# Moving the softmax attention's query projection from filling work into a pass of seven half-size products

## The chip, the cores and the metric

The kernel runs on one core of one Trainium2 chip. A core has engines that run side by side and wait for each other by semaphores: TensorE (PE, matrix products, with PEld for its weight loads), VectorE (DVE), ScalarE (ACT), GpSimd (POOL), and SyncE (SP), whose queue issues the transfers between DRAM and the on-chip memory SBUF. Products land in PSUM, in eight banks. The metric is the device time of one execution in microseconds (us). Less is better.

## The reference, cut to what matters

One encoder layer over 1024 tokens of width 1024, in float32. An input projection gives everything that the two attention branches need; branch A is gated linear attention (GLA) in both directions, branch B is softmax attention over a window (SWA).

```python
h = _rms_norm(x, norm_mix_g[l])
proj = h @ w_in[l]
(g_q, g_k, g_v, g_r, g_lr_f, g_lr_b,
 s_q, s_k, s_v, gate_a, gate_b) = jnp.split(proj, split_at, axis=-1)
y_gla = _gla_branch(g_q, g_k, g_v, g_r, ...) @ w_o_gla[l]
y_swa = _swa_branch(s_q, s_k, s_v, ...) @ w_o_swa[l]
merged = sigmoid(gate_a) * y_gla + sigmoid(gate_b) * y_swa
x = x + merged @ w_out[l]
x = x + (silu(ff_gate) * ff_up) @ w_ffn_out[l]
```

The change is about four parts of `proj`: `g_v` (GLA values, 1024 columns), `s_q` (SWA queries, 1024 columns), `s_k` with `s_v` (SWA keys and values, 256 columns each), and `g_r` (1024 columns, used only when branch A's output is gated).

## The kernel before, in words

**Precision.** Every large product is made of three matmuls in the fast type fp32r: each operand is split into a high part (ScalarE copies it to fp32r) and a low part (VectorE subtracts the high part from the original), and high x high, high x low and low x high are summed in PSUM. One matmul takes a 128x128 block of one operand and streams 512 columns of the other. `wunit` (L67) makes one weight unit of 128x512: SP loads 256 KB, ScalarE copies (L70), VectorE subtracts (L72).

**Stages, in the order of the program.** First come projections by a scheme with seven instead of eight half-size products (0 to 249.6 us in the profile). Then `values()` (L516 to L561) makes `g_v` the same way: seven products of `vproduct` (L474 to L483), each of four weight units on four PSUM banks, three matmuls each, so 48 matmuls a product and 336 in all, on line L482. Two groups of four banks take turns: `A` from the `ch` banks, `B` from the `mm` banks. The finished blocks are split into high and low and stored to DRAM by `vkeep` (L488).

Then the GLA stage (325.8 to about 555 us) runs in slots. A table `at` (L862 on) says which step of which chunk (`g_gates`, `g_powers`, `g_scores`, `g_out`, `g_back_out`, `g_turn`, and `k_norm` of the softmax keys) stands in which slot. There are 4 heads of 8 chunks, slots 0 to 45. The order of TensorE's instructions is the order in which the program writes them; the other engines' order is left to the scheduler. Between the steps `slot` (L212) calls `fill(n)`, which puts in n matmuls of a list `dense` of projections that nothing waits for soon: `skv` (192 matmuls), `sq0` and `sq1` (192 each, the softmax queries), and `r0` to `r7` (48 each), 960 in all. The fillings split their weights by `wunit`: one unit for 12 matmuls of `proj_t` (skv, sq0, sq1), and one for 24 of `proj_f` (r0 to r7). Finished blocks leave PSUM by ScalarE (`proj_t`, L189, 8 copies of 128x512 in 192 matmuls) or by VectorE (`proj_f_out`, L128, 2 in 48).

The SWA stage (about 555 to 738 us) has a table `todo` of the same kind: for each of 16 units of 4 heads, `a_load`, `a_prep` (normalise and rotate the queries, VectorE), `a_turn` (L970, transposes), `a_scores` (products, maximum, exponential, and on GpSimd the division, L1008), and two slots later `a_probs` and `a_out`. It goes on filling, and `fill(1 << 30)` after it puts in what is left. From 738 us on come the output projections and the feed-forward part, which the change does not touch.

**How many matmuls a slot gets.** GLA: `fill(24)` first, then 24 in slots 0 and 1, 16 in slots 2 and 3, 12 in slots 4 to 35, 8 in slots 36 to 43, 18 in slots 44 and 45 (L878). SWA: 26 in slots 0 and 1, 15 in slots 2 to 18, 18 after (L1084).

**What the steps of a chunk do on the small engines.** `g_scores` (L719) scales two query blocks by a decay (`q2f`, `q2b`, VectorE, L746) and splits the scores into `sh` (VectorE, L750) and `sl` (VectorE, L751). `k_norm` (L834) normalises and rotates the keys of one tile of 128 tokens, eight calls. `g_back_out` (L787) ends with a pair of scaled outputs `ob` (ScalarE, L805), which `g_turn` (L807) transposes on TensorE (L811), copies and stores (L815).

Of the kernel before, what the change touches and what calls it, by code (L numbers as in the profile page):

```python
# [8 lines left out]
F32 = mybir.dt.float32  # L9
# [5 lines left out]
P = 128  # L15
# [15 lines left out]
def body(tc, i, out):  # L31
    nc = tc.nc
    with ExitStack() as root:
# [102 lines left out]

        def next_unit():
            while plan and len(ready) <= AHEAD:
                ready.append(wunit(plan.pop(0)))
            return ready.pop(0)  # L140

        def proj_f(name, m):
            plan.extend(i["w_f"][m, u] for u in range(2))
# [17 lines left out]
        def proj_t(name, n):  # L161
            for s in range(2):
                plan.extend(i["w_t"][n, k] for k in range(KT))
# [287 lines left out]
        def x_last(f):  # L451
# [9 lines left out]
                 "12": ("xr00", "xr20", "xr21", "xr10"), "u": ("wr2", "wr2", "wr2", "rsl"), "p": ("ws",) * 4}  # L461

# [5 lines left out]

        def vload(q, k):
            nc.sync.dma_start(out=vtile(q, k), in_=i["w_t"][int(q[0]) - 1, 4 * int(q[1]) - 4 + k])  # L470
# [4 lines left out]
        def vproduct(ys, w, x, start, stop, after):  # L475
            for kk in range(4):
# [6 lines left out]
                after(kk)  # L483

# [31 lines left out]
        def values():  # L516

            A = [chtile((P, HT)) for _ in range(4)]
# [5 lines left out]
            vproduct(A, lambda k: wunit(i["w_t"][0, k]), X0["11"], True, False, early)  # L524
            for m in range(4):
                vcopy("p", m, A[m], m)
            B = [mmtile() for _ in range(4)]
# [6 lines left out]
            vproduct(B, lambda k: wunit(i["w_t"][0, 4 + k]), X0["21"], True, True, sums)  # L534
# [6 lines left out]
            B = [mmtile() for _ in range(4)]  # L541
# [11 lines left out]
            vproduct(A, vsplit_of("11"), X0["T3"], False, False, restore)  # L553
# [6 lines left out]
            for m in range(4):  # L560
                vkeep(1, m, A[m], True)  # L561

        with tc.manual_schedule(engines={mybir.EngineType.PE}):
# [60 lines left out]
            values()  # L624
# [99 lines left out]
        def g_scores(hd, c):  # L724
# [18 lines left out]
            for d, on in ((0, c > 0), (1, c < NC - 1)):  # L743
                if on:
                    q = a.pr.q2[d][:, a.t]
                    nc.vector.tensor_scalar(q, q, decay(hd, c, d), None, op0=ALU.mult)  # L746
# [3 lines left out]
            nc.vector.tensor_copy(a.sh, sp)  # L750
            nc.vector.tensor_tensor(a.sl, sp, a.sh.bitcast(F32), op=ALU.subtract)  # L751

# [54 lines left out]
        def g_turn(hd, c):  # L807
# [6 lines left out]
            for j in range(2):  # L814
                nc.sync.dma_start(out=scr["o", 2 * hd + j, c // 4][:, (c % 4) * P:(c % 4 + 1) * P], in_=os_[:, j])  # L815
# [18 lines left out]
        def k_norm(t):  # L834

            need(("skv", t))
            raw = gtile("kvr", (P, 2, P))
            nc.sync.dma_start(out=raw.rearrange("p a b -> p (a b)"), in_=scr["skv", t][:, 0:256])
            b = gtile("sq2", (P, 2, P), bufs=1)
            ss = gtile("ss2", (P, 2))  # L840
            nc.scalar.activation(b, raw, AF.Square)
            nc.vector.tensor_reduce(ss, b, axis=mybir.AxisListType.X, op=ALU.add)
            rs = gtile("rs2", (P, 2))
            rsqrt(rs, ss, 1.0 / 128, EPS, epst, gt, (P, 2), "sn2")
            qn = gtile("qn2", (P, 2, P))
            for h in range(2):
                nc.vector.scalar_tensor_tensor(qn[:, h], raw[:, h], rs[:, h:h + 1], tb[0], op0=ALU.mult, op1=ALU.mult)
            c = tb[1][:, t:t + 1].to_broadcast([P, 2, 64])
            s = tb[2][:, t:t + 1].to_broadcast([P, 2, 64])
            nc.vector.tensor_tensor(b[:, :, 0:64], qn[:, :, 64:128], s, op=ALU.mult)  # L850
            nc.vector.tensor_tensor(b[:, :, 64:128], qn[:, :, 0:64], s, op=ALU.mult)
            nc.vector.tensor_tensor(qn[:, :, 0:64], qn[:, :, 0:64], c, op=ALU.mult)
            nc.vector.tensor_tensor(qn[:, :, 64:128], qn[:, :, 64:128], c, op=ALU.mult)
# [844 lines left out]
```

## Time and profile before

| what | value |
|---|---|
| times of three runs | 1624.68, 1624.97, 1625.12 us |
| median | 1624.97 us |
| span of the profiled execution | 1623.5 us |
| TensorE busy | 1613.2 us (99%) |
| VectorE busy | 1277.7 us (79%) |
| ScalarE busy | 820.3 us (51%) |
| GpSimd busy | 76.4 us (5%) |
| `values()`, first to last matmul | 249.6 to 325.8 us |
| GLA stage, to the last transposes of its output | 325.8 to 554.8 us |
| SWA stage, from the first transposes of queries to the end of filling | 572.0 to about 738 us |

The span is the profiled execution from its first to its last instruction, and the runs lie 1.2 to 1.6 us above it. In the views a line names when an instruction starts, how long it takes, its engine, line and operation, what it writes and reads, and, in brackets, how long the engine was idle ahead of it and who ended that. A view by windows gives the busy time of each engine in a stretch, with the number of instructions in brackets, the granted clock of TensorE (1.00 is full), the busy share of the 16 DMA engines and what they moved. Consecutive matmuls of 512 columns start 0.227 us apart where nothing stops them, although each is shown as 0.39 us long, since they overlap.

### The profile page before, as it was taken

The numbers are of one execution on the slowest core, as the hardware profiler recorded it, in microseconds if no ns is written. First come the engines' busy times: TensorE is split into PE (matmuls) and PEld (weight loads), VectorE is DVE, ScalarE is ACT, GpSimd is POOL, SyncE is SP. The second block draws the span as 40 slices with busy tenths as digits, with TensorE's granted clock in tenths as the row PEclk, the third lists the DMA queues.
The fourth block names the chain that finished last, engine by engine and source line by source line (L and its number), as shares of the span: only waits on it lengthen the run. The fifth ranks groups of instructions, "written<-read, shape, count | busy, mean of one in ns | idle before, by whom it ended". The sixth has DMA issues, their size and how long they took to land.

```text
span 1623.5 us, 23271 instructions
## 1 busy us (share of the span) xinstructions
PE 1613.2 (99%) x7540; PEld 1338.9 (82%) x7540; DVE 1277.7 (79%) x2663; ACT 820.3 (51%) x1700; POOL 76.4 (5%) x68
## 2 busy tenths in 40 slices
PE   9999999999999999999999999999999999999999
PEld 7888888888888778888888888888888888888887
DVE  8888775589998499966887769887777888789655
ACT  8643334466787577665445546333333333354442
POOL 0000000000000035440000000000000000000000
PEclk9999999999999999999999999999999999999999
DMA  7664444486554543248867654453234444596433
GB/s 238 183 236 150 132 135 156 150 268 185 169 175 144 191 120 116 79 143 289 279 201 230 197 162 128 130 173 109 95 104 146 147 143 148 175 344 190 150 97 117
DMA packets 176778, 272.88 MB, mean 168 GB/s; under 512 B 23996, under 2 KB 57532, under 8 KB 176656
## 3 DMA queue, kind: packets, MB, share of 16 engines
q1 hardware_dynamic: 176656, 271.39, 52.3%
q8 instruction: 60, 0.98, 0.3%
q14 instruction: 62, 0.51, 0.1%
HBM read 194.75 MB, written 76.56 MB: 167 GB/s over the span
## 4 chain that ended last, share of the span: by engine, by line
PE 82%; DVE 11%; DMA 3%; ACT 2%; issue 1%; SPq 1%; DVEq 0%; ACTq 0%
PE mm L76 15%; PE mm L312 10%; PE mm L311 10%; PE mm L313 10%; PE ch L76 7%; PE mm L1511 7%; PE ch L1511 6%; PE ch L312 4%; PE ch L313 4%; PE ch L311 4%; PE ch L482 3%; PE mm L482 2%; DVE wl L72 1%; PE ch L1019 1%; DVE cs L683 1%
## 5 line engine op out<-in xcount | busy, mean ns | idle before, releaser
L303 ACT ACTIVATE wh<-ws 128x512 fp32r<-128x512 f32 x132 | 83.4, 632 | 149.1 <-PE mm L312 88.4
L70 ACT ACTIVATE wh<-wr 128x512 fp32r<-128x512 f32 x182 | 113.1, 628 | 69.4 <-PE mm L76 31.2
L72 DVE TENSOR_TENSOR wl<-wr,wh 128x512 fp32r<-128x512 f32 x182 | 124.1, 685 | 25.4 <-ACT wh L70 24.1
L1008 POOL TENSOR_SCALAR p<-p,rd 128x384 f32<-128x384 f32 (+1 forms) x64 | 76.2, 1208 | 646.3 <-DMA kvr<-skv 583.3
L304 DVE TENSOR_TENSOR wl<-ws,wh 128x512 fp32r<-128x512 f32 x132 | 90.4, 686 | 19.8 <-ACT wh L303 19.7
L303 ACT ACTIVATE wh<-wr 128x512 fp32r<-128x512 f32 x69 | 43.6, 632 | 119.5 <-issue 56.0
L303 ACT ACTIVATE wh<-a 128x512 fp32r<-128x512 f32 x64 | 40.5, 633 | 91.0 <-PE ch L1511 42.3
L76 PE MATMUL mm<-wh,xl 128*128 128x512 f32 x192 | 83.3, 434 | 0.0
L76 PE MATMUL mm<-wh,xh 128*128 128x512 f32 x192 | 79.6, 415 | 0.0
L76 PE MATMUL mm<-wl,xh 128*128 128x512 f32 x192 | 79.2, 413 | 0.0
L304 DVE TENSOR_TENSOR wl<-a,wh 128x512 fp32r<-128x512 f32 x64 | 44.2, 691 | 43.0 <-ACT wh L303 42.5
L1511 PE MATMUL mm<-hh,wh 128*128 128x512 f32 x176 | 68.5, 389 | 0.0
L1511 PE MATMUL mm<-hl,wh 128*128 128x512 f32 x176 | 68.5, 389 | 0.0
L1511 PE MATMUL mm<-hh,wl 128*128 128x512 f32 x176 | 68.5, 389 | 0.0
L76 PE MATMUL mm<-xh,wh 128*128 128x512 f32 x160 | 64.7, 405 | 0.1
L76 PE MATMUL mm<-xl,wh 128*128 128x512 f32 x160 | 64.4, 403 | 0.1
L76 PE MATMUL mm<-xh,wl 128*128 128x512 f32 x160 | 59.8, 408 | 0.0
L1481 DVE TENSOR_TENSOR hl<-hr,hh 128x512 fp32r<-128x512 f32 x75 | 51.4, 685 | 3.9 <-ACT hh L1480 3.9
L1511 PE MATMUL ch<-hh,wh 128*128 128x512 f32 x132 | 51.3, 389 | 0.0
L1511 PE MATMUL ch<-hl,wh 128*128 128x512 f32 x132 | 51.3, 389 | 0.0
L1511 PE MATMUL ch<-hh,wl 128*128 128x512 f32 x132 | 51.3, 389 | 0.0
L76 PE MATMUL mm<-mh,wl 128*128 128x512 f32 x128 | 49.9, 390 | 0.9 <-DVE wl L72 0.9
(676 smaller groups left out, 5087.2 us busy)
## 6 DMA issues: line engine op xcount, KB each, us to landing
wr<-in_w_fi_dram SPq DMA_DIRECT2D x102, 256.0 KB, 2.9
wr<-in_w_f_dram SPq DMA_DIRECT2D x80, 256.0 KB, 3.2
wr<-in_w_t_dram SPq DMA_DIRECT2D x56, 256.0 KB, 3.4
B<-c SPq DMA_DIRECT2D x44, 256.0 KB, 2.1
T<-tx SPq DMA_DIRECT2D x44, 256.0 KB, 3.1
a<-in_w_fo_dram SPq DMA_DIRECT2D x44, 256.0 KB, 5.4
hr<-T SPq DMA_DIRECT2D x44, 256.0 KB, 2.6
wr<-in_w_oa_dram SPq DMA_DIRECT2D x32, 256.0 KB, 3.9
```

What stands on the lines that cost most here:

```text
L70: nc.scalar.activation(h, raw, AF.Copy)
L72: nc.vector.tensor_tensor(l, raw, h.bitcast(F32), op=ALU.subtract)
L76: nc.tensor.matmul(o, a, b, start=start, stop=stop)
L303: nc.scalar.activation(h, src, AF.Copy)
L304: nc.vector.tensor_tensor(l, src, h.bitcast(F32), op=ALU.subtract)
L311: nc.tensor.matmul(o, h[:, c], x[kk][0], start=start and kk == 0, stop=False, skip_group_check=True)
L312: nc.tensor.matmul(o, h[:, c], x[kk][1], start=False, stop=False, skip_group_check=True)
L313: nc.tensor.matmul(o, l[:, c], x[kk][0], start=False, stop=kk == nk - 1, skip_group_check=True)
L482: nc.tensor.matmul(ys[m], a[:, c], b, start=f0, stop=f1, skip_group_check=True)
L1008: nc.gpsimd.tensor_scalar(p[:, h, :w], p[:, h, :w], rd[:, h:h + 1], None, op0=ALU.mult)
L1481: nc.vector.tensor_tensor(l, r, h.bitcast(F32), op=ALU.subtract)
L1511: nc.tensor.matmul(ys[m], a[:, c], b, start=f0, stop=f1, skip_group_check=True)
```

## The change

It has five parts.

1. `sq0` and `sq1` leave the filling. `values` now takes arguments and runs twice: once for the GLA values as before, and once for the softmax queries (`base` 3), again 7 products of 48 matmuls. In the second pass the groups of banks are swapped (`A` from `mm`, `B` from `ch`), and `vkeep` stores each finished block once, unsplit; the last four blocks go through a ScalarE copy first.
2. The weights of the remaining filling (8 units of skv, 16 of r0 to r7) are split ahead: `split_one`, twice in every product of the two passes until the 24 units are done, makes a unit by `wunit` and stores its high and low part to DRAM (256 KB each). The filling then loads both parts (`kept_unit`) and needs no ScalarE or VectorE for them.
3. The slots get fewer fillings: GLA 16, 12, 7, 4, 12 (were 24, 16, 12, 8, 18), SWA 14, 8, 17 (were 26, 15, 18).
4. In `g_scores` the scaling of `q2b` and the copy `sh` go from VectorE to ScalarE. `k_norm` takes two tiles at a time with wide operands: four calls, 30 VectorE instructions where there were 72, and 16 scalings on ScalarE.
5. The scratch memory for dynamic transfers is set to 1024 bytes.

```diff
+        def kept_unit(key):
+            u = []
+            for j in range(2):
+                t = wp.tile([P, 512], FR, tag=("wh", "wl")[j], name=nm("wf"), bufs=5)
+                nc.sync.dma_start(out=t.bitcast(F32), in_=scr["w", *key, j])
+                u.append(t)
+            return u
+
         def next_unit():
             while plan and len(ready) <= AHEAD:
-                ready.append(wunit(plan.pop(0)))
+                ready.append(kept_unit(plan.pop(0)))
             return ready.pop(0)
...
+        split_ahead = [("t", 2, k) for k in range(KT)] + [("f", 8 + m, u) for m in range(KT) for u in range(2)]
+
+        def split_one():
+            if split_ahead:
+                key = split_ahead.pop(0)
+                for j, t in enumerate(wunit(i["w_" + key[0]][key[1:]])):
+                    d = scratch("w%s%d_%d_%d" % (*key, j))
+                    nc.sync.dma_start(out=d, in_=t.bitcast(F32))
+                    scr["w", *key, j] = d
...
                 after(kk)
+                if kk % 2:
+                    split_one()
...
         def vkeep(n, ti, c, direct=False):
+            if vbase[0]:
+                if direct:
+                    t = w0.tile([P, 512], F32, tag="ws", name=nm("vc"), bufs=4)
+                    nc.scalar.activation(t, c, AF.Copy, scale=rstdt[:, ti:ti + 1])
+                    c = t
+                d = scratch(f"sq{n}_{ti}")
+                nc.sync.dma_start(out=d, in_=c)
+                scr[f"sq{n}", ti] = d
+                return
...
-        def values():
-
-            A = [chtile((P, HT)) for _ in range(4)]
+        def values(base, one, two, last):
+
+            vbase[0] = base
+            A = [one() for _ in range(4)]
...
-            B = [mmtile() for _ in range(4)]
+            B = [two() for _ in range(4)]
...
-            values()
+            values(0, lambda: chtile((P, HT)), mmtile, False)
+            values(3, mmtile, lambda: chtile((P, HT)), True)
...
-            for d, on in ((0, c > 0), (1, c < NC - 1)):
-                if on:
-                    q = a.pr.q2[d][:, a.t]
-                    nc.vector.tensor_scalar(q, q, decay(hd, c, d), None, op0=ALU.mult)
+            if c:
+                q = a.pr.q2[0][:, a.t]
+                nc.vector.tensor_scalar(q, q, decay(hd, c, 0), None, op0=ALU.mult)
...
-            nc.vector.tensor_copy(a.sh, sp)
+            nc.scalar.activation(a.sh, sp, AF.Copy)
             nc.vector.tensor_tensor(a.sl, sp, a.sh.bitcast(F32), op=ALU.subtract)
+            if c < NC - 1:
+                q = a.pr.q2[1][:, a.t]
+                nc.scalar.activation(q, q, AF.Copy, scale=decay(hd, c, 1))
...
-        dense += [proj_t("skv", 2), proj_t("sq0", 3),
-                  proj_t("sq1", 4)] + [proj_f(f"r{m}", 8 + m) for m in range(8)]
+        dense += [proj_t("skv", 2)] + [proj_f(f"r{m}", 8 + m) for m in range(8)]
...
-                n = 24 if t < 2 else 16 if t < 4 else 12 if t < NH * NC + 4 else 8 if t < last - 1 else 18
+                n = 16 if t < 2 else 12 if t < 4 else 7 if t < NH * NC + 4 else 4 if t < last - 1 else 12
...
-                slot([lambda e=e: e[0](*e[1:]) for e in v], 26 if t < 2 else 15 if t < 2 * KT + 3 else 18)
+                slot([lambda e=e: e[0](*e[1:]) for e in v], 14 if t < 2 else 8 if t < 2 * KT + 3 else 17)
```

**What moves on the engines.** The first place is TensorE near the end of the GLA stage, where a head's outputs are finished backwards: `ob` transposes (`ident,ob`), products of the running state (`kb,q2b`), and fillings (the `mm` rows). Before, the kernel had:

```order
2402 L76 MATMUL mm_6231<-wh_6407,xh_96 128x512
2403 L76 MATMUL mm_6231<-wl_6409,xh_96 128x512
2404 L811 MATMUL ch_6578<-ident,ob_1461_6060 128x128 x2
2405 L76 MATMUL mm_6231<-wh_6407,xl_112 128x512
2406 L76 MATMUL mm_6232<-wh_6407,xh_96 128x512
2407 L76 MATMUL ch_6587<-kb_1439_5989,q2b_1302_5532 128x256
2408 L76 MATMUL mm_6232<-wl_6409,xh_96 128x512
2409 L76 MATMUL mm_6232<-wh_6407,xl_112 128x512
2410 L76 MATMUL mm_6233<-wh_6407,xh_96 128x512
2411 L76 MATMUL mm_6233<-wl_6409,xh_96 128x512
2412 L76 MATMUL ch_6634<-kb_1409_5882,q2b_1244_5336 128x256
```

At the same place it now has:

```order
2534 L76 MATMUL mm_6642<-xh_99,wf_6358 128x512
2535 L846 MATMUL ch_6955<-ident,ob_1555_6553 128x128 x2
2536 L76 MATMUL mm_6642<-xl_115,wf_6358 128x512
2537 L76 MATMUL ch_6963<-kb_1536_6492,q2b_1417_6094 128x256
2538 L76 MATMUL mm_6643<-xh_100,wf_6358 128x512
2539 L76 MATMUL mm_6643<-xl_116,wf_6358 128x512
2540 L76 MATMUL ch_6982<-kb_1509_6397,q2b_1362_5918 128x256
```

Between the two products with `kb` stood four fillings and now stand two; the fillings read weights as loaded (`wf`), and they belong to an `r` projection instead of `sq1`.

The second place is VectorE in the middle of the GLA stage, around the scores of one chunk. Before, with the two decays (L746), a weight split (L72) and the copy `sh` (L750):

```order
654 L746 TENSOR_SCALAR q2f_4211<-q2f_4211,dec_4202 128x128
655 L104 TENSOR_SCALAR rt_4424<-oss_4313 128x2
656 L746 TENSOR_SCALAR q2b_912_4212<-q2b_912_4212,dec_4375 128x128
657 L737 TENSOR_TENSOR ktl_4441<-ch_4437,kth_4440 128x256
658 L105 TENSOR_TENSOR rt_4424<-rt_4424,rl_4421 128x2
659 L747 COPY_PREDICATED sp_4447<-tri,ch_4444 128x128
660 L106 SCALAR_TENSOR_TENSOR rt_4424<-rt_4424,rl_4421 128x2
661 L72 TENSOR_TENSOR wl_4596<-wr_4592,wh_4594 128x512
662 L107 SCALAR_TENSOR_TENSOR ors_4420<-rt_4424,rl_4421 128x2
663 L750 CAST sh_4452<-sp_4447 128x128
664 L762 SCALAR_TENSOR_TENSOR pf_4465<-pf_4358,dec_4044,ch_4458 128x256
665 L751 TENSOR_TENSOR sl_4453<-sp_4447,sh_4452 128x128
```

Now:

```order
744 L105 TENSOR_TENSOR rt_5437<-rt_5437,rl_5434 128x2
745 L770 TENSOR_TENSOR ktl_5453<-ch_5449,kth_5452 128x256
746 L106 SCALAR_TENSOR_TENSOR rt_5437<-rt_5437,rl_5434 128x2
747 L779 COPY_PREDICATED sp_5459<-tri,ch_5456 128x128
748 L107 SCALAR_TENSOR_TENSOR ors_5433<-rt_5437,rl_5434 128x2
749 L797 SCALAR_TENSOR_TENSOR pf_5476<-pf_5378,dec_5052,ch_5469 128x256
750 L711 TENSOR_SCALAR e_5495<-e_5495 128x512
751 L819 SCALAR_TENSOR_TENSOR kb_1203_5380<-kb_1231_5478,dec_5052,kb_1203_5380 128x256
752 L778 TENSOR_SCALAR q2f_5403<-q2f_5403,dec_5394 128x128
753 L819 SCALAR_TENSOR_TENSOR kb_1180_5308<-kb_1203_5380,dec_5052,kb_1180_5308 128x256
754 L783 TENSOR_TENSOR sl_5464<-sp_5459,sh_5463 128x128
```

The weight split, the decay of `q2b` and the copy `sh` are gone from VectorE's queue.

The third place is SP's queue while the values' results are stored. Before, the stores of the high and low parts (`vh`, `vl`) stood one behind the other:

```order
206 L505 DMA vh_4_2933<-vh_2929 128x512
207 L505 DMA vh_5_2942<-vh_2938 128x512
208 L505 DMA vl_4_2935<-vl_2930 128x512
209 L505 DMA vl_5_2944<-vl_2939 128x512
210 L505 DMA vh_6_2951<-vh_2947 128x512
211 L505 DMA vl_6_2953<-vl_2948 128x512
```

Now loads and stores of the units split ahead (`wr`, `wf_`) and loads of the second pass's weights (`v_`) stand between them:

```order
243 L535 DMA vh_7_3036<-vh_3032 128x512
244 L535 DMA vl_7_3038<-vl_3033 128x512
245 L68 DMA wr_3072<-in_w_f_dram 128x512
246 L68 DMA wr_3114<-in_w_f_dram 128x512
247 L477 DMA wf_0_0_3078<-wh_3074 128x512
248 L477 DMA wf_0_1_3080<-wl_3076 128x512
249 L477 DMA wf_1_0_3120<-wh_3116 128x512
250 L489 DMA v_714_3482<-in_w_t_dram 128x512
251 L477 DMA wf_1_1_3122<-wl_3118 128x512
252 L489 DMA v_665_3302<-in_w_t_dram 128x512
253 L489 DMA v_671_3326<-in_w_t_dram 128x512
254 L489 DMA v_719_3505<-in_w_t_dram 128x512
```

Each row is a transfer of 256 KB.

More of the change, by code (lines that the diff above doesn't have):

```diff
@@ L834, in k_norm @@
         def k_norm(t):
[L836 to L840, printed above, removed]
+            raw = gtile("kvr", (P, 2, 2, P))
+            for j in range(2):
+                need(("skv", t + j))
+                nc.sync.dma_start(out=raw[:, j].rearrange("p a b -> p (a b)"), in_=scr["skv", t + j][:, 0:256])
@@ L861, in body @@
+            table(t // 2)
         at = {}
```

62 lines of the change are left out of this document (36 added, 26 removed).

## The prediction

> **What bounds the kernel now.** I read the busy times first, then the windows cut at the stages' borders, then TensorE's timeline at those borders. The page says that TensorE is hardly ever free:
>
> ```profile
> PE 1613.2 (99%) x7540; PEld 1338.9 (82%) x7540; DVE 1277.7 (79%) x2663; ACT 820.3 (51%) x1700; POOL 76.4 (5%) x68
> ```
>
> An average over stages hides who else is full. The windows show that; each row gives the stretch, its length, and the busy time of PE, PEld, DVE, ACT and POOL, then clock, transfers' share and rate:
>
> ```profile
> 249.60:325.80 76.20, 76.20 (x338) 63.08 (x336) 40.34 (x64) 34.02 (x56) 0.00 (x0) 1.00 0.42 145
> 325.80:344.70 18.90, 18.90 (x86) 15.38 (x85) 14.64 (x33) 10.03 (x19) 0.00 (x0) 1.00 0.92 299
> 344.70:515.10 170.40, 169.02 (x983) 144.42 (x982) 166.15 (x617) 125.12 (x364) 0.00 (x0) 1.00 0.60 179
> 515.10:554.90 39.80, 39.51 (x202) 32.87 (x201) 19.51 (x60) 29.15 (x83) 0.00 (x0) 1.00 0.46 146
> 554.90:572.00 17.10, 15.69 (x72) 12.39 (x70) 7.82 (x20) 6.07 (x16) 0.00 (x0) 1.00 0.83 270
> 572.00:640.90 68.90, 68.11 (x377) 57.88 (x378) 68.71 (x225) 50.14 (x139) 32.70 (x27) 1.00 0.36 109
> 640.90:738.00 97.10, 96.58 (x518) 81.63 (x517) 74.67 (x225) 62.12 (x157) 43.47 (x38) 1.00 0.41 123
> 738.00:1623.50 885.50, 880.76 (x3881) 728.17 (x3879) 685.41 (x1102) 374.51 (x651) 0.00 (x0) 1.00 0.53 170
> ```
>
> In the values' pass (first row) TensorE is alone at its limit: VectorE has 40 of 76 us. In the middle of the GLA stage (third row) TensorE and VectorE are both full (169.0 and 166.2 of 170.4), and again in the first half of the SWA stage (sixth row, 68.1 and 68.7 of 68.9). So the change takes TensorE's work out of stages where VectorE stands right behind, and pays for it in one where only TensorE counts. The last row, 885.5 us, stays as it is.
>
> Starts of TensorE's instructions give the prices:
>
> ```profile
> 249.62 0.39 PE L482 MATMUL ch<-wh,xh 128*128 128x512 f32 x1
> ...
> 325.55 0.39 PE L482 MATMUL ch<-wh,T4l 128*128 128x512 f32 x1
> 325.78 0.39 PE L76 MATMUL mm<-wh,xh 128*128 128x512 f32 x1
> ...
> 331.46 0.40 PE L76 MATMUL ch<-lrS,upS 98*128 98x256 f32 x2
> ...
> 344.69 0.38 PE L733 MATMUL ch<-ident,en 128*128 128x128 f32 x2
> ...
> 542.01 0.59 PE L76 MATMUL ch<-kb,q2b 128*128 128x256 f32 x2
> ...
> 545.64 0.38 PE L811 MATMUL ch<-ident,ob 128*128 128x128 f32 x2
> ...
> 554.76 0.38 PE L811 MATMUL ch<-ident,ob 128*128 128x128 f32 x2
> ...
> 566.07 0.41 PE L947 MATMUL ch<-ident,key 128*128 128x128 f32 x2 [0.69 <-ACT vSh L941]
> ...
> 572.00 0.66 PE L970 MATMUL ch<-ident,qn 128*128 128x128 f32 x4 [0.72 <-DVE qn L964]
> ```
>
> From the first row to the third, 336 products take 76.16 us, 0.2267 us each. That is the price of a filling too.
>
> **The change part by part.** If only TensorE counted, 384 fillings leave (-87.0 us) and 336 products come (+76.2): -10.9. The rest is about how much of the 87.0 really goes. By the slots' numbers the GLA stage loses 2x8 + 2x4 + 32x5 + 8x4 + 2x6 = 228 fillings, the SWA slots 2x12 + 17x7 + 3x1 = 146, and the remainder put in at the end 10.
>
> *Second pass:* +76.2.
>
> *Its end:* the last four blocks now lie in the `mm` banks that the first filling wants, and each bank comes free by a ScalarE copy:
>
> ```profile
> L189 ACT ACTIVATE st<-mm,rstdt 128x512 f32<-128x512 f32 x24 | 16.7, 694 | 3.2 <-PE mm L76 3.0
> ```
>
> The end of the last product (0.39 less the 0.23 by which the next would have started) and 0.69 for one copy, with a little for the semaphores, give +1.1; bounds 0 (the first bank is free early) and 2.5 (three copies end ahead of it). Before, the fillings went on 0.23 us after the last product.
>
> *Transfers in the first pass:* the rate before is 145 GB/s, so 11.0 MB. Some 42 transfers of `split_one` and 16 early loads for the second pass, 262 KB each, add 15.2 MB: 26.2 MB in 76 us is 344 GB/s. The fastest long stretches are
>
> ```profile
> 320.00:330.00 10.00, 10.00 (x45) 8.01 (x44) 5.13 (x8) 4.51 (x8) 0.00 (x0) 1.00 0.91 328
> 1420.00:1450.00 30.00, 30.00 (x134) 24.82 (x134) 23.97 (x38) 17.80 (x30) 0.00 (x0) 1.00 1.04 387
> ```
>
> both with TensorE never waiting. At 387 it takes 68 us and hides; at 328 it takes 80 us, 4 more than the pass. The early loads can slip into the second pass, which has fewer stores, so I take +2, bounds 0 and +8 (twice the excess, if SP's queue, in order, holds a load behind a store that waits for its data). VectorE and ScalarE gain 14 splits there, 14 x 0.68 = 9.5 us on 40 and 9 on 34 of 76: hidden.
>
> *GLA, opening* (second window): 16 fillings, 3.6 us. The stretch is a chain from the gates at 331.46 to the transposes at 344.69; its last steps on VectorE are
>
> ```profile
> 339.66 0.42 DVE L715 TENSOR_TENSOR q2f<-cs,qk 128x256 f32<-128x256 f32 x1
> ```
>
> and the next, done by about 340.4. So TensorE comes 4.3 us after its data; 3.6 fits nearly, I take 2.7.
>
> *GLA, middle:* 8 + 29 slots x 5 = 153 fillings, 34.7 us; TensorE needs 135.7 of the 170.4. VectorE must fall as far. Its queue, with nothing between (start to start):
>
> ```profile
> 448.73 0.28 DVE L746 TENSOR_SCALAR q2b<-q2b,dec 128x128 f32<-128x128 f32 x1
> 448.92 0.15 DVE L105 TENSOR_TENSOR rt<-rt,rl 128x2 f32<-128x2 f32 x1
> ...
> 449.73 0.22 DVE L750 CAST sh<-sp 128x128 fp32r<-128x128 f32 x1
> 449.86 0.68 DVE L72 TENSOR_TENSOR wl<-wr,wh 128x512 fp32r<-128x512 f32 x1
> 450.46 0.28 DVE L751 TENSOR_TENSOR sl<-sp,sh 128x128 fp32r<-128x128 f32 x1
> ```
>
> A decay costs 0.19, `sh` 0.13, a split 0.60. Over the whole stage and in `k_norm` the groups are
>
> ```profile
> L72 DVE TENSOR_TENSOR wl<-wr,wh 128x512 fp32r<-128x512 f32 x52 | 35.4, 686 | 10.7 <-ACT wh L70 10.5
> L847 DVE SCALAR_TENSOR_TENSOR qn<-kvr,rs,kg 128x128 f32<-128x128 f32 x16 | 5.2, 349 | 0.2
> ```
>
> Of the 52 splits about 31 (375 fillings by 12) lie in the middle, 18.6 us; 28 decays are 5.4, 32 copies 4.2, and `k_norm` gives about 4 (its 16 scalings of 5.2 go to ScalarE, wider tables take part of that back). Together 32.2, so VectorE comes to 134 and TensorE to 136. Two engines that close do not overlap without loss; before, TensorE lost 1.4 us there. I take -33. ScalarE takes over some 60 small copies and loses 31 splits, so its 125 falls.
>
> *GLA, tail:* 56 fillings, 12.7 us. Here a pair of outputs has a chain: the `kb` product at 542.01, addition, norm, then the scaling
>
> ```profile
> 544.92 0.91 ACT L805 ACTIVATE ob<-ob,ors 128x256 f32<-128x256 f32 x2
> ```
>
> which frees the transposes of 545.64. That is 3.4 us to the first scaled half; the program now gives TensorE about 2.2 us of other work (two products of 0.43 and six fillings). Some 1.3 us at each of three pairs, and -8.4 is left. GLA together: -2.7 - 33 - 8.4 = **-44.1**, bounds -51 (all 225 fillings) and -36 (VectorE's middle gains only its splits, decays and copies at a third less, and the tail half).
>
> *Join* (fifth window): the next chain needs no filling. After the last transposes at 554.76 come
>
> ```profile
> 555.77 0.81 SPq L815 DMA_DIRECT2D o<-ot  x2
> ...
> 562.71 0.43 SPq L937 DMA_DIRECT2D qr<-sq  x1
> ```
>
> with ten other issues of SP between them, then the queries' data
>
> ```profile
> 567.58 0.63 ACT L913 ACTIVATE sq<-qr 128x512 f32<-128x512 f32 x1 [0.38 <-DMA qr<-sq]
> ```
>
> and VectorE's rotation, until `qn` at 572.00. TensorE already waited 0.69 and 0.72 us at its two stops; 30 fillings (6.8 us) fewer are only longer waits. **0**, bounds -6.8 and +1.
>
> *SWA, first half* (sixth window, eight slots): 56 fillings, 12.7 us, but VectorE was busy 68.7 of 68.9, and loses only what the fillings gave it:
>
> ```profile
> L72 DVE TENSOR_TENSOR wl<-wr,wh 128x512 fp32r<-128x512 f32 x17 | 11.6, 683 | 9.4 <-ACT wh L70 9.4
> L128 DVE TENSOR_TENSOR st<-mm,rstd 128x512 f32<-128x512 f32 x15 | 10.0, 684 | 7.5 <-DMA key<-key 4.3 <-PE mm L76 3.0 <-DMA bw<-in_w_ob_dram 0.2
> ```
>
> 120 fillings had 5 splits (one in 24) and 5 blocks out (two in 48); 64 have no split and 2.7 blocks: 7.3 x 0.60 = 4.4. I take **-4.5**, bounds -12.7 and -2. *Second half:* VectorE had 22 us to spare; 73 fillings, 16.5 us, of which I take **-14.5**, bounds -16.5 and -11, since the chain over GpSimd from scores to probabilities now has less work above it.
>
> The sum: 76.2 + 1.1 + 2 - 44.1 + 0 - 4.5 - 14.5 = +16.2. On the span of 1623.5 that gives 1639.7; the median of the runs lies 1.5 above the span, so the time is 1624.97 + 16.2 = **1641.2 us**.
>
> One rule speaks against such a change. The Trainium skill, page "Perfetto Trace Analysis", section "Optimization Strategy", says that where the most contended engine changes over time, interleaving those regimes may be faster. The trace agrees that the regimes differ (VectorE 40 of 76 us in one window, 68.7 of 68.9 in another), and the change separates what was interleaved; by the rule alone the sign would be mine, by the count of TensorE's work alone -10.9.
>
> **The rivals.** *TensorE sets the pace everywhere (faster).* VectorE's busy time overstates it: the split above is 0.68 long but the next starts after 0.60. Over 225 instructions of the sixth window, up to 0.08 each is 18 us, and VectorE's real need may be near 51 rather than 68.7. If a slot there needs less than (68.9 - 12.7)/8 = 7.0 us of VectorE, all fillings count, and if the join's chain shortens too: 76.2 + 1.1 - 51 - 6.8 - 29.2 = -9.7, 1615.3 us. Against it: no gap of the first half was left unused, and the join's chain is one of transfers. If the join stays, -2.9, 1622.1: no change that can be told.
>
> *Transfers bind in the passes (slower still).* At 250 GB/s, between the 145 before and 328, the 26.2 MB need 105 us, and half of the 29 us excess slips into the second pass: 14.5 in place of my 2, so 1653.7. For it: SP's queue is in order and stores wait there; against it: 387 GB/s was moved.
>
> *The clock drops.* All rows above have clock 1.00 and no wait over 0.72 us. In the join TensorE would now idle twice, 6.8 us less 1.4 or so each way, perhaps 3 to 5 us at a time. Were the next 14 fillings (14 x 0.2267 = 3.2 us) to run at half speed each time, that is +6.4: 1647.6.
> The Trainium skill, page "TensorE: Matmul & The Clock Gate", section "What's actually happening", states such a rule, half clock after an idle window of about 3.4 us and full again after about as long; no run here shows it yet.
>
> **How the numbers follow.** My forecast has 0.50, the fast rival 0.22, its variant with the join unchanged 0.10, transfers 0.10, the clock 0.08. About 0.2% (3.2 us) is what a measurement of this kernel can tell from no change. The forecast's own bounds reach from 1625 (GLA at -51, first half at -12.7) to 1652, and a little of it falls near no change: faster 0.22, same 0.11, slower 0.67. The range takes in the fast rival down to 1613 and the slower ones up to 1652, leaving out half of the two slow rivals and a part of the fast one.
>
> **What would show it.** In the changed profile: a second row of 336 products, about 76 us, with TensorE without a wait and transfers above 300 GB/s in the first pass (right) or with waits for loads (transfers). The GLA stage from the passes' end to the last `ident,ob` should take 185 us (229 before); 178 says the fast rival. From there to the first `ident,qn` 17 us with several us of TensorE idle, or 10. The first eight SWA slots 64 us with VectorE above 97% busy, or 56 with TensorE full. A granted clock below 1.00 after the join would be the last rival. I am wrong if VectorE shows idle time in the first half of the SWA stage while TensorE is full there.

## The result, and the profile after

The changed kernel takes 1670.62 us (1667.75 to 1674.18) against 1625.05: a ratio of 1.0286 (interval 1.0273 to 1.0298), 45.6 us slower. The forecast had the sign, and about a third of the size: 1641.2, and 1652.0 at most. The profiled execution has a span of 1668.6 us, 45.1 more than before.

The windows of the changed kernel, cut at the same events as before (both passes; GLA to the first transposes of `en`, to the last, to the last of `ob`; the join; the first eight SWA slots, the next seven), columns as in the prediction:

```profile
249.78:417.74 167.96, 158.29 (x673) 128.43 (x672) 93.66 (x146) 73.87 (x122) 0.00 (x0) 0.97 0.74 255
417.74:432.34 14.60, 14.60 (x68) 12.08 (x67) 5.83 (x17) 4.12 (x8) 0.00 (x0) 1.00 0.93 311
432.34:570.67 138.33, 134.90 (x830) 115.63 (x829) 133.57 (x474) 119.98 (x387) 0.00 (x0) 1.00 0.68 206
570.67:601.89 31.22, 27.62 (x148) 22.82 (x147) 14.65 (x51) 19.85 (x66) 0.00 (x0) 1.00 0.42 133
601.89:618.39 16.50, 10.17 (x41) 7.76 (x40) 5.28 (x15) 4.11 (x10) 0.00 (x0) 0.90 0.83 266
618.39:686.46 68.07, 57.75 (x320) 47.20 (x320) 65.55 (x219) 47.72 (x134) 32.56 (x27) 1.00 0.36 109
686.46:752.49 66.03, 57.69 (x304) 46.91 (x304) 51.76 (x176) 41.35 (x112) 34.08 (x30) 0.97 0.22 65
```

| stretch | before | after | difference | forecast |
|---|---|---|---|---|
| passes of seven products | 76.2 | 168.0 | +91.8 | +79.3 |
| GLA, opening / middle / tail | 18.9 / 170.5 / 39.7 | 14.6 / 138.3 / 31.2 | -4.3 / -32.2 / -8.4 | -2.7 / -33 / -8.4 |
| join | 17.1 | 16.5 | -0.6 | 0 |
| SWA, first eight slots | 68.9 | 68.1 | -0.9 | -4.5 |
| SWA, next seven | 64.8 | 66.0 | +1.3 | the rest of the stage: -14.5 |
| all after that | 917.8 | 916.2 | -1.7 | |

Two stretches went wrong: the passes lost 15.6 us beyond 672 products at 0.2267, and the SWA stage gave back nothing. Of the 28.9 us by which the forecast missed the span, 12.5 lie in the passes and 17.7 in the SWA stage with what follows it. TensorE is busy only 57.75 of 68.07 us in its first half, so the fillings did leave; the slots stayed nearly as long.

Where the passes lost it, in TensorE's timeline in the sixth product of the first pass:

```profile
309.17 0.39 PE L501 MATMUL mm<-wl,xh 128*128 128x512 f32 x1
309.40 0.39 PE L501 MATMUL mm<-wh,xl 128*128 128x512 f32 x1
314.04 0.79 PE L501 MATMUL mm<-wh,xh 128*128 128x512 f32 x1 [4.25 <-ACT wh L311]
314.85 0.80 PE L501 MATMUL mm<-wl,xh 128*128 128x512 f32 x1
315.44 0.63 PE L501 MATMUL mm<-wh,xl 128*128 128x512 f32 x1
```

The product's own weights (`wh`, L311) come late from ScalarE. ScalarE's timeline says why:

```profile
306.95 0.63 ACT L531 ACTIVATE vh<-vp 128x512 fp32r<-128x512 f32 x1 [1.83 <-DVE vp L543]
312.84 0.63 ACT L70 ACTIVATE wh<-wr 128x512 fp32r<-128x512 f32 x1 [5.25 <-DMA wr<-in_w_f_dram]
313.37 1.13 ACT L311 ACTIVATE wh<-v 128x512 fp32r<-128x512 f32 x2
```

Ahead of L311 stands L70, the copy of a unit split ahead, and it waits 5.25 us for its load. And SP's queue says why the load is late:

```profile
298.19 1.65 SPq L489 DMA_DIRECT2D v<-in_w_t_dram  x2
303.79 1.01 SPq L535 DMA_DIRECT2D vh<-vh  x2
...
308.34 0.32 SPq L535 DMA_DIRECT2D vl<-vl  x1
308.75 1.27 SPq L68 DMA_DIRECT2D wr<-in_w_f_dram  x2
```

The load (L68) is issued behind eight stores of the values' parts, which themselves wait for the results of the fifth product. It happens again in the seventh product (3.42 us). After each wait TensorE runs at half its clock for a while; around the first one, in windows of 4 us:

```profile
308.00:312.00 4.00, 1.79 (x8) 1.13 (x7) 0.31 (x1) 0.00 (x0) 0.00 (x0) 0.97 0.92 324
312.00:316.00 4.00, 1.95 (x4) 1.26 (x5) 2.50 (x5) 3.08 (x6) 0.00 (x0) 0.50 0.42 159
316.00:320.00 4.00, 4.00 (x14) 3.18 (x13) 1.20 (x2) 0.27 (x1) 0.00 (x0) 0.68 0.90 264
```

In the SWA stage the waits of TensorE are many and short (engine, what waits, releaser: total us, times, longest):

```profile
PE ch L76 <- ACT sob L1075: 4.5, 7, 1.4
PE ch L1061 <- POOL p L1050: 4.4, 6, 1.2
PE ch L76 <- DVE kTl L992: 3.3, 2, 1.7
PE ch L76 <- DVE pl L1065: 3.1, 7, 0.9
PE ch L76 <- DVE mx L1030: 2.8, 5, 0.8
```

No one releaser carries it: the PSUM banks `ch` that ScalarE (`sob`) and VectorE (`pl`, `mx`) have to empty, and GpSimd's division (`p`).

### The profile page after: what moved, and what is told of

It is laid out like the page before. It is cut to its first block, busy times and chain, and to the rows that moved or that the text cites. A ratio compares the mean times of both kernels' runs of the same rounds, so it can differ in the third digit from the quotient of the medians.

```text
span 1668.6 us, 23252 instructions
## 1 busy us (share of the span) xinstructions
PE 1619.1 (97%) x7492; PEld 1333.6 (80%) x7492; DVE 1273.0 (76%) x2561; ACT 834.2 (50%) x1752; POOL 76.1 (5%) x68
## 4 chain that ended last, share of the span: by engine, by line
PE 77%; DVE 12%; ACT 4%; DMA 4%; issue 1%; POOL 1%; SPq 0%; ACTq 0%; DVEq 0%
PE mm L76 11%; PE mm L321 9%; PE mm L319 9%; PE mm L320 9%; PE mm L1553 7%; PE ch L1553 5%; PE ch L76 5%; PE ch L321 4%; PE ch L320 4%; PE ch L319 4%; PE ch L501 4%; PE mm L501 4%; ACT p L1044 1%; DVE cs L716 1%; DMA wr<-in_w_f_dram 1%
## 5 line engine op out<-in xcount | busy, mean ns | idle before, releaser
L311 ACT ACTIVATE wh<-ws 128x512 fp32r<-128x512 f32 x132 | 83.4, 632 | 147.4 <-PE mm L320 87.6
L70 ACT ACTIVATE wh<-wr 128x512 fp32r<-128x512 f32 x150 | 93.0, 627 | 83.2 <-PE mm L76 23.1
L72 DVE TENSOR_TENSOR wl<-wr,wh 128x512 fp32r<-128x512 f32 x150 | 102.5, 689 | 38.0 <-ACT wh L70 37.8
L311 ACT ACTIVATE wh<-wr 128x512 fp32r<-128x512 f32 x69 | 43.6, 632 | 120.0 <-issue 56.5
L76 PE MATMUL mm<-xh,wf 128*128 128x512 f32 x256 | 101.9, 437 | 0.0
L311 ACT ACTIVATE wh<-a 128x512 fp32r<-128x512 f32 x64 | 40.5, 632 | 90.7 <-PE ch L1553 42.3
L76 PE MATMUL mm<-xl,wf 128*128 128x512 f32 x128 | 54.9, 429 | 0.0
L76 PEld LDWEIGHTS mm<-xh,wf 128*128 128x128 f32 x256 | 48.5, 192 | 5.2
L76 PE MATMUL mm<-mh,wh 128*128 128x512 f32 x128 | 49.8, 389 | 0.0
L76 PE MATMUL mm<-ml,wh 128*128 128x512 f32 x128 | 49.8, 389 | 0.0
L1044 ACT ACTIVATE p<-p,nm,rs 128x384 f32<-128x384 f32 (+1 forms) x64 | 42.9, 671 | 11.7 <-DVE nm L1038 5.9
```

The costliest lines, as they stand in the source:

```text
L70: nc.scalar.activation(h, raw, AF.Copy)
L72: nc.vector.tensor_tensor(l, raw, h.bitcast(F32), op=ALU.subtract)
L76: nc.tensor.matmul(o, a, b, start=start, stop=stop)
L311: nc.scalar.activation(h, src, AF.Copy)
L1044: nc.scalar.activation(p[:, h, :w], p[:, h, :w], AF.Exp, bias=nm_[:, h:h + 1], scale=a.rs[:, h:h + 1], accum_out=dn[:, h:h + 1])
```

## The experiments

Stages are given as in the table above. The changed kernel's four runs span 6 us, and stages that an edit leaves alone differ by 1 to 3 us between the profiles, of which there is one for each experiment; smaller differences are not read. First four runs asked what holds each of the two stretches.

**Late splitting.** In the changed kernel, no unit is split ahead in the last two products of the first pass; the second pass makes them.

```diff
-        def vproduct(ys, w, x, start, stop, after):
+        def vproduct(ys, w, x, start, stop, after, ahead=True):
...
-                if kk % 2:
+                if kk % 2 and ahead:
                     split_one()
...
-            vproduct(B, vsplit_of("12"), X0["22"], False, True, lambda k: None)
+            vproduct(B, vsplit_of("12"), X0["22"], False, True, lambda k: None, last)
...
-            vproduct(A, vsplit_of("22"), X0["T4"], False, True, lambda k: None)
+            vproduct(A, vsplit_of("22"), X0["T4"], False, True, lambda k: None, last)
```

> The changed kernel without the units split ahead in the last two products of the first pass; all 24 are still made, in the first five products of the first pass and all seven of the second. Theory 'queue': the 15.6 us that the two passes took over 152.4 come from ScalarE's in-order queue, where the copy of a unit split ahead waits for a load that SP can only issue behind the stores of vh and vl, with the product's own weights queued behind it, and from the halved clock after each such wait. Then the two passes take 152.5 to 155 us (168.0 before), no granted clock below 1.00 in them, and the time is 1655 to 1658. Rival 'rate': the DMA engines are full; the bytes of the two passes are the same here, the waits only move, and the time is within 4 us of 1670.6.

Measured: 1656.61 us, 14.0 less than the changed kernel. The passes:

```profile
249.05:403.31 154.26, 153.14 (x673) 125.99 (x672) 93.08 (x146) 73.52 (x122) 0.00 (x0) 1.00 0.80 274
```

154.3 us, the clock at 1.00, with the same transfers at a higher mean rate (274 against 255 GB/s). A load of a weight unit (L68) landed 3.8 us after its issue in both kernels (median of those recorded), and the late one above was in use 4.1 us after its issue. So the order of the queues was the cause, and not the rate of the transfers.

**Fewer fillings in the kernel before**, SWA slots alone.

```diff
-... 26 if t < 2 else 15 if t < 2 * KT + 3 else 18)
+... 14 if t < 2 else 8 if t < 2 * KT + 3 else 17)
```

> The kernel before with nothing changed but the fillings of the SWA slots: 14, 8, 17 where there were 26, 15, 18. The 146 fillings taken out are put in at the end. Theory 'own chain': the SWA stage is held by its own work (VectorE in the first half, the chain over ScalarE and GpSimd in the second), so its first to last transposes of queries stay at 131 to 135 us (133.7) and the time is 1651 to 1658. Rival 'filling paced' (the one of the prediction): the stage gives back 14 to 24 us and the time is 1634 to 1642 at most.

Measured: 1657.74 us, 32.6 more than before; the stage from first to last transposes of queries took 134.7 us (133.7 before):

```profile
574.31:709.03 134.72, 117.72 (x621) 96.85 (x622) 119.18 (x395) 90.82 (x249) 64.31 (x55) 0.96 0.27 82
```

What follows these slots got 31.1 us longer, of the 33.1 us of the 146 fillings. In the kernel before, the fillings cost next to nothing where they stood.

**No fillings in the SWA slots of the changed kernel.**

```diff
-... 14 if t < 2 else 8 if t < 2 * KT + 3 else 17)
+... 0)
```

> The changed kernel with no fillings at all in the SWA slots; those 215 come at the end (48.7 us). Theory 'own chain': first to last transposes of queries take 122 to 134 us (134.4 with fillings; VectorE loses about 6 blocks of 0.6 us), and the time is 1705 to 1718. Rival 'filling paced': the stage gets shorter by 8 fillings in each of 15 slots, 27 us, to 107, and the time is about 1675 to 1690.

Measured: 1715.89 us; the stage 138.2 us, with nothing to fill it:

```profile
618.75:690.70 71.95, 52.82 (x252) 42.33 (x253) 64.41 (x217) 47.55 (x134) 32.36 (x27) 0.86 0.24 72
690.70:757.00 66.30, 51.57 (x248) 40.87 (x247) 48.57 (x166) 40.68 (x110) 32.42 (x29) 0.89 0.15 45
```

That is 4 us slower than with fillings, and above the 122 to 134 expected. TensorE's clock was 0.86 to 0.89 there, so a part of the length may be the clock; what the stage would take without fillings at full clock is not shown. It did not get shorter: with 15, 8 or no fillings in a slot it takes 134 to 138 us.

**Without the division**, the first look at what holds it. The normalisation of the softmax is left out.

```diff
-            for h in range(4):
-                nc.gpsimd.tensor_scalar(p[:, h, :w], p[:, h, :w], rd[:, h:h + 1], None, op0=ALU.mult)
```

> The changed kernel without GpSimd's division of the probabilities by their sum (left out, so the softmax is not normalised). Theory 'own chain': in the second half of the SWA stage the 4.9 us on GpSimd stand in a chain from scores to probabilities; the last seven slots (686.5 to 752.5, 66.0 us) get shorter by 8 to 15 us, the first eight (68.1 us) by less than 3, since VectorE is full there; the time is 1655 to 1663. Rival 'VectorE throughout': the whole stage changes by less than 3 us.

Measured: 1662.47 us; the first eight slots 66.1 (-2.0), the next seven 60.0 (-6.0). GpSimd is a part of it in the second half, less than expected.

**Without half of the rotation**, to test VectorE. The queries' rotation is left out in part.

```diff
-            nc.vector.tensor_tensor(b[:, :, 0:64], qr[:, :, 64:128], ...
-            nc.vector.tensor_tensor(b[:, :, 64:128], qr[:, :, 0:64], ...
             nc.vector.tensor_tensor(a.qn, qr, qA[:, n:n + 1].to_broadcast([P, 4, P]), op=ALU.mult)
-            nc.vector.tensor_tensor(a.qn, a.qn, b, op=ALU.add)
```

> The changed kernel with half of the queries' rotation left out (two products and the addition on VectorE, 1.3 us a slot). Theory 'VectorE holds the first half': the first eight SWA slots, 68.1 us with VectorE busy 65.6, get shorter by 7 to 11 us, the next seven (66.0) by 0 to 4. Rival 'banks or latency throughout': both halves change by less than 3 us.

Measured: 1671.72 us, no gain. The first and the second half:

```profile
618.92:689.65 70.73, 60.91 (x320) 49.37 (x319) 54.05 (x194) 47.45 (x134) 33.09 (x28) 0.96 0.34 106
689.65:753.56 63.91, 56.66 (x303) 45.95 (x302) 44.12 (x154) 41.35 (x112) 31.04 (x28) 0.99 0.22 67
```

VectorE is 11.5 us less busy in the first half (54.05, it was 65.55), and the half is 2.7 us longer. My theory that VectorE holds it fell here: a busy share of 96% was no bound.

**VectorE's relief in the GLA stage undone**: `sh` and the decay of `q2b` back on VectorE.

```diff
-            nc.scalar.activation(a.sh, sp, AF.Copy)
+            nc.vector.tensor_copy(a.sh, sp)
...
-                nc.scalar.activation(q, q, AF.Copy, scale=decay(hd, c, 1))
+                nc.vector.tensor_scalar(q, q, decay(hd, c, 1), None, op0=ALU.mult)
```

> The changed kernel with the decay of q2b and the copy sh back on VectorE, as in the kernel before. Theory: the middle of the GLA stage (138.3 us from first to last transposes of en) is now set by VectorE, and 28 decays of 0.19 and 32 copies of 0.13, 9.5 us, come back nearly whole: the middle takes 144 to 149 us and the time is 1676 to 1681. Rival: TensorE still sets it, the middle changes by less than 3 us.

Measured: 1670.68 us, no change. The middle of GLA and its tail:

```profile
431.86:570.02 138.16, 134.15 (x831) 115.84 (x830) 136.72 (x517) 103.99 (x317) 0.00 (x0) 1.00 0.65 200
570.02:602.00 31.98, 27.86 (x149) 22.80 (x148) 19.86 (x67) 22.66 (x76) 0.00 (x0) 1.00 0.50 155
```

The middle is as long as it was. But not all of the 9.5 us was added to it: all 28 decays and 31 of the 32 copies are back on VectorE there, yet it has only 43 instructions more (517 against 474) and is busy 3.2 us more (136.7 against 133.6). The difference is some 15 instructions of `k_norm` and the tables, which now run in the tail (16 more there, and 5.2 us more of busy time). Middle and tail together grew by 0.6 us. So the stage as a whole had room for this work, and VectorE did not set its time; what the middle would take with all of it added is not shown. TensorE is busy 134 of 138 us.

**Fillings moved from GLA to SWA**, on top of late splitting.

```diff
-... 16 if t < 2 else 12 if t < 4 else 7 if t < NH * NC + 4 else 4 if t < last - 1 else 12
+... 16 if t < 2 else 12 if t < 4 else 4 if t < NH * NC + 4 else 2 if t < last - 1 else 4
...
-... 14 if t < 2 else 8 if t < 2 * KT + 3 else 17)
+... 26 if t < 2 else 15 if t < 2 * KT + 3 else 18)
```

> The run with late splitting (1656.6 us; GLA stage 185.4 us, SWA 133.9 from first to last transposes of queries), with fillings moved from GLA to SWA: GLA slots 16, 12, 4, 2, 4 (were 16, 12, 7, 4, 12), SWA 26, 15, 18 as in the kernel before. Theory 'own chain': 15 fillings in a SWA slot are free (SWA stays at 132 to 137 us); the GLA stage, where VectorE is busy 97 to 100% in the middle, gives back 4 to 12 us of the 28 us of TensorE's work taken out; the time is 1644 to 1653. Rival 'paced by TensorE': GLA loses 26 to 28 us and SWA gains as much; no change within 3 us of 1656.6.

Measured: 1651.95 us, 4.7 less. GLA fell by 14.7 us to 170.7, more than expected; SWA rose by 5.4 to 139.3, a little above the 132 to 137 expected, and the join by 2.3. Fillings in SWA slots are nearly free, and taking them out of the GLA stage pays only in part (14.7 of 28 us).

**Eight banks instead of four**: no fillings in SWA, and the scores in the free `mm` banks.

```diff
-            s = chtile((P, 384))
+            s = mmtile((P, 384))
...
+            for _ in dense.pop(0):
+                pass
...
-... 14 if t < 2 else 8 if t < 2 * KT + 3 else 17)
+... 0)
```

> The changed kernel with no fillings in the SWA slots, as in the run without them (138.2 us from first to last transposes of queries: 72.0 in the first eight slots, 66.2 in the next seven), and the scores in the four mm banks that are then free, so that the four ch banks serve only transposes and outputs. The projection under way is finished ahead of the SWA stage. Theory 'banks': in the second half TensorE, in order, waits for one of four ch banks that ScalarE or VectorE has still to empty; with twice the banks those seven slots take 50 to 59 us, the first eight 64 to 70 (VectorE was busy 64.4 us there), and the time is 1697 to 1708. Rival 'latency': the chain from scores to probabilities holds the slots whatever the banks; both halves stay within 3 us of 138.2 in sum.

Measured: 1727.45 us; the stage 148.8 us instead of 138.2. The waits for banks are nearly gone, and one other has taken their place (from 618 to 757 us):

```profile
PE ch L1061 <- POOL p L1050: 26.3, 30, 1.9
PE ch L1012 <- DVE qn L1006: 5.6, 1, 5.6
PE ch L989 <- ACT vSh L983: 5.3, 1, 5.3
```

Both expectations failed: banks alone do not hold the stage, and it got 10.6 us longer, at a clock of 0.82. The next look was at the order of the small engines' queues. One slot of the changed kernel, ScalarE:

```profile
650.31 0.71 ACT L1044 ACTIVATE p<-p,nm,rs 128x384 f32<-128x384 f32 x1 [0.48 <-DVE rt L106]
...
653.19 0.56 ACT L1075 COPY sob<-ch 128x512 f32<-128x512 f32 x1
653.66 1.55 ACT L1064 ACTIVATE ph<-ch 128x512 fp32r<-128x512 f32 x3
```

And VectorE in the same slot:

```profile
654.29 1.88 DVE L1065 TENSOR_TENSOR pl<-ch,ph 128x512 fp32r<-128x512 f32 x3
656.09 0.55 DVE L1030 CUSTOM_DVE_ANT_0 p<-ch,band 128x384 f32<-128x384 f32 x1
...
659.79 0.14 DVE L1038 SCALAR_TENSOR_TENSOR nm<-sink,mx 128x4 f32<-128x4 f32 x1
```

The exponentials of one unit, the output copy and `ph` behind them, `pl` behind `ph`, the next unit's maxima behind `pl`, `nm`, and the next exponentials: from 650.31 to about 659.9 the round closes in 9.6 us. That was my next theory, with two runs that put the same work on the round and off it.

**The output copy three times** (on the round):

```diff
-            nc.scalar.copy(ob, o)
+            for _ in range(3):
+                nc.scalar.copy(ob, o)
```

> The changed kernel with ScalarE's copy of a unit's output, sob, made three times instead of once (about 0.5 us each, so 1.0 us a unit more on ScalarE). Theory 'loop through the queues': a SWA slot is as long as one round of exponentials, output copy, ph, pl, maxima, exponentials, each standing behind the one before it in the in-order queues of ScalarE and VectorE; work in that round counts in full whatever the engines' busy share. Then the stage from first to last transposes of queries (134.1 us) gets 11 to 28 us longer (0.75 to 1.9 a slot) and the time is 1680 to 1699. Rival 'busy time': ScalarE is busy 6 of 9 us in a slot, so 1 us fits: less than 4 us longer.

**The squares three times** (off the round, `inv_norm`):

```diff
-            nc.scalar.activation(sq, raw[:, 0:n], AF.Square)
+            for _ in range(3):
+                nc.scalar.activation(sq, raw[:, 0:n], AF.Square)
```

> The control for the tripled output copy: the changed kernel with the squares of the queries (0.6 us each) made three times, about 1.1 us a unit more on ScalarE, at a place where ScalarE waits 2 us for the next transposes. Theory 'loop through the queues': this is not in the round, the stage (134.1 us) stays within 5 us and the time within 1667 to 1676. Rival 'ScalarE's work counts wherever it stands': as with the output copy, 11 us or more.

Measured: 139.1 us with the copies (+5.0; 1675.56 us), 133.4 with the squares (-0.7; 1673.15 us). In the stage the same 1 us of ScalarE's work costs something at one place and nothing at the other, as the theory said; the two times, 2.4 us apart, hardly separate the runs. And the copies cost 0.3 us a slot, not 0.75 to 1.9: the simple round overstates it.

**Two other orders**: `ph`, `pl` and the output copy scheduled at high priority, or the maxima.

```diff
+            with tc.high_priority():
                 nc.scalar.activation(ph, pt, AF.Copy)
                 nc.vector.tensor_tensor(pl, pt, ph.bitcast(F32), op=ALU.subtract)
...
+            with tc.high_priority():
                 nc.scalar.copy(ob, o)
```

> The changed kernel with a higher scheduling priority for ph, pl and the output copy, which puts them ahead of or between the exponentials in the queues of ScalarE and VectorE (E E q o E h h h E and the like). Theory 'loop': the order of the queues sets the slot, so the stage's 134.1 us change by 4 us or more, and get shorter (116 to 130 us) if the PSUM banks that TensorE waits for come free earlier; the time is then 1652 to 1667. Rival: the order does not matter, within 3 us of 134.1.

```diff
+            with tc.high_priority():
                 nc.vector.tensor_tensor_reduce(out=p[:, h, :w], in0=s[:, :w], in1=band[:, mo:mo + w],
```

> The changed kernel with a higher scheduling priority for the maxima of the scores on VectorE, which puts them between the pl (M l M l M M l) where they stood behind them (l l l M M M M). Theory 'loop': up to 1.2 us leave the round (two of three pl), the stage's 134.1 us get 4 to 16 us shorter, and the time is 1655 to 1667. Rival: the order does not matter, within 3 us of 134.1.

Measured: 142.5 us (+8.4; 1683.68 us) and 132.2 us (-1.9; 1668.42 us; the first half 3.4 longer, the second 5.3 shorter). The first of them has 18.0 us of waits for GpSimd between 618 and 753 us, the second stays within the rival's 3 us. Order matters, but neither order shortens the round as the theory in its simple form said.

**Both constraints off**, which was still open: the runs without fillings, with four or eight banks, now without the division as well (left out as above).

> The changed kernel with no fillings in the SWA slots (138.2 us from first to last transposes of queries) and without GpSimd's division (left out, so the softmax is not normalised). With the two runs that had eight banks, this makes a square: banks four or eight, division or none. Theory 'two rounds': with four banks the round through the banks holds the slots, so leaving out the division alone gives 4 to 14 us (124 to 134). Rival 'GpSimd alone': 100 to 115.

> The run with the scores in the mm banks and no fillings in the SWA slots (148.8 us, with 26 us of waits for GpSimd), without the division as well (left out). Theory 'two rounds', one through the banks and the queues of ScalarE and VectorE, one through GpSimd: with both gone the stage takes 100 to 122 us, more of a gain than either alone. Rival 'order of the queues': the poor order of that run stays, 135 or more.

| first to last transposes of queries, no fillings | division | no division |
|---|---|---|
| four banks | 138.2 | 123.0 |
| eight banks | 148.8 | 115.3 |

More banks help only where the division is gone (-7.7), and with it they make things worse (+10.6); the division is worth 15.2 us with four banks and 33.5 with eight. Taking away the limit of banks alone gave nothing, the division alone 15.2 us (just more than expected), both 22.9. That fits two rounds side by side, one over the `ch` banks and the queues of ScalarE and VectorE, one over GpSimd. It is argued from four sums, not shown: moving the scores to other banks may also reorder the queues, and TensorE's clock was 0.82 to 0.91 in all four runs. (Times: 1699.95 and 1685.37 us.)

**The change mended as far as found**: late splitting, fillings moved, maxima at high priority.

> The run with fillings moved to the SWA slots and late splitting (1652.0 us, stage 139.3), with the maxima at a higher scheduling priority as well. If the priority helps as in the changed kernel: 1646 to 1651. It does not reach the kernel before (1625), since the second pass costs 78 us and the stages give back at most 60.

Measured: 1652.96 us, just above the 1646 to 1651 expected, the stage 137.1. The priority adds nothing here. No version reached the kernel before.

## Why the prediction was wrong

- **Second pass, +76.2:** near; it took 79.0 us (338.76 to 417.74), the first pass 89.0. With late splitting both together took 154.3 us, 1.9 above 672 products at full pace.
- **Its end, +1.1:** 0. The first filling starts 0.227 us after the last product. The banks of the last product end 0.68 us apart (three matmuls each), so the first copy starts at 415.90, is 0.7 long, and is done before the filling at 417.75 needs it; I had let all four end together.
- **Transfers, +2 (0 to +8):** failed; +15.6 instead. The prediction priced bytes against a rate. The bytes did fit: in the run with late splitting TensorE waited about 1 us over both passes. What counted was that a copy which nobody needs soon stood in ScalarE's in-order queue ahead of one that TensorE needed, waiting for a load that stood in SP's in-order queue behind stores. Of the 15.6 us, two waits (4.4 and 3.6 us from start to start beyond the usual step) make 8.0, the steps after them, most at the halved clock, 4.7 (11 steps from 309.40 to 318.74 take 9.34 us, 6.85 more than at 0.2267, and 12 steps from 327.16 to 335.75 lose 5.9), the rest, 2.9, is short waits. The rival on transfers (slower still) had the place, and its 14.5 us lies near the 15.6, but it priced bandwidth: that its size came close was luck.
- **GLA, -44.1:** -44.9, each part near its forecast. (The tail's own terms, 12.7 less three times 1.3, come to 8.8; 8.4 was written and measured.) The reason given for the middle was too strict: VectorE need not have fallen as far as TensorE. With 9.5 us of its removed work put back (by start-to-start prices), middle and tail together grew by 0.6 us, since other work of VectorE could move into the tail. Whether the split weights were needed for it was not tried.
- **Join, 0:** -0.6. The chain from the last outputs to the first queries sets it. TensorE idled 5.0 us there and the clock stood at 0.90, as the rival on the clock said, but the transposes wait for the chain anyway and it cost nothing that can be seen.
- **SWA, -4.5 and -14.5:** failed; +0.4 over fifteen slots, and -1.7 over all that follows. The step that failed is "VectorE had 22 us to spare; 73 fillings, 16.5 us, of which I take -14.5". It read the slack of the busiest small engine as room for TensorE. Shown: the stage takes 134 to 139 us with 15, 8 or no fillings in a slot; 11.5 us less work on VectorE in the first half gave nothing. TensorE's 99% before was in part fillings that covered waits: with 146 of them taken out of the kernel before, it was idle 17.0 of 134.7 us. The first half's -4.5 rested on VectorE as the bound, which fell too.
- **The fast rival** rested on the same reading (busy time of VectorE overstates it, so TensorE paces). Its first part was borne out in the SWA stage (96% busy, and no bound), its conclusion not. The first eight slots showed neither of the two pictures named: 68.1 us, with VectorE at 96% and TensorE at 85%.

What stays open is what holds a SWA slot, and how much each place in the two rounds has of it; the sum of one round in the queues, 9.6 us in the slot shown, lies near the 8.9 us of a mean slot, but does not explain the sizes of the runs that changed it.

## What to carry to other kernels

Fillings that keep an engine at 99% say nothing of what their stage would take without them: before moving such work to a place where it costs full price, take it out of the stage alone and see whether the stage gets shorter. One such run (146 fillings fewer, +32.6 us) would have told the outcome in the SWA stage, though not the waits in the passes. Work that is done ahead needs its loads issued ahead as well: behind a late load on an in-order engine stands everything that is urgent.

## What the runs showed of the hardware

**TensorE's clock.** After TensorE had waited 4.25 us, consecutive matmuls started 0.43 us apart instead of 0.227 until 4.4 us after the wait, and the granted clock read 0.50. After 3.42 us the clock still read 1.00 for the first 1.2 us and then 0.50, with starts 0.43 us apart, until 4.4 us after the wait. The Trainium skill, page "TensorE: Matmul & The Clock Gate", section "What's actually happening", gives an idle window of about 3.4 us for this and as long to come back; the trace agrees in the main for these two waits.

Shorter waits can do it too. From 748.67 to 752.07 us the changed kernel's clock read 0.50 after waits of 1.36 and 0.19 us, with TensorE busy 1.85 of the 3.41 us before; after a wait of 1.22 us at 725.30 it stayed at 1.00. In the run without fillings, no wait in the second half of the SWA stage was longer than 1.9 us, and the mean clock there was 0.89.

**VectorE's busy share.** A share near 100% did not show that VectorE set the time: in the first eight SWA slots it was busy 65.55 of 68.07 us, and with 11.5 us less the slots took 70.73.
